# A two-layer diffusion block: layer 0's FFN in one pass over all tokens, or in two passes, context first

## The chip, the cores and the metric

The kernel runs on one core of a Trainium2 chip. The metric is the device time of one execution in microseconds (us). The core has five engines with a queue of instructions each: PE (matmuls; its weight loads are listed as PEld), DVE (vector), ACT (activations, casts, copies), POOL (a second vector engine) and SP, which here issues nearly all DMAs. An engine takes its instructions strictly in order: one that waits holds up all behind it.

## The reference

Two layers over 512 latent and 256 context tokens of width 1024. Each layer is a mixer (layer 0: windowed attention with a sink beside a dense grouped one; layer 1: differential attention) and a SwiGLU FFN with 2816 hidden columns. Before each mixer and each FFN stands an RMS norm with a shift and a scale, behind each a gate; these six vectors per layer ("modulation", parts 0 to 5) come from the conditioning vectors. Only the latents are returned, so layer 1 computes no FFN for the context.

```python
for l in range(DEPTH):
    mx = silu(c) @ mod_w[l] + mod_b[l]; mc = silu(c_ctx) @ mod_w[l] + mod_b[l]
    shx1, scx1, gx1, shx2, scx2, gx2 = split(mx, 6)    # the same for mc
    x = x + gx1 * mixer(rms(x) * (1 + scx1) + shx1, ...)
    x = x + gx2 * swiglu(rms(x) * (1 + scx2) + shx2, ffn_w_in[l], ffn_w_out[l])
    # the context likewise with mc, but in layer 0 only
def swiglu(h, w_in, w_out):
    gate, up = split(h @ w_in, 2)
    return (silu(gate) * up) @ w_out
```

## The kernel before

Tokens lie in six tiles of 128: t = 0 to 3 are latents, 4 and 5 the context. Every fp32 operand of a matmul is split into a high and a low fp32r part, and every product is three matmuls (high·high, low·high, high·low). ACT casts the high part (wbh, wdh, hdh), DVE or POOL subtracts it for the low part (wbl, wdl, hdl). Weights are loaded by SP as fp32 into raw buffers (wgr, wur, wr, wdr, modw) first.

The stages follow one another: layer 0's mixer, its FFN ("FFN 0"), layer 1's mixer ("mixer 1"), FFN 1. The normed tokens stand transposed in SBUF, latents as hT (512 columns), context as hTc (256).

**FFN 0** is the function `ffn`. It goes over the 22 slices f of 128 hidden columns in pairs p. For each f it forms gate (pg) and up (pu) products over eight K tiles, latents and context side by side (L814), then the hidden tile `silu(pg) * pu`, split. After every pair (the last two pairs together) the down products dps (L869 to L871) go over all tokens, and `residual` (L439, L440) multiplies by the gate row g and adds to the token tile x in SBUF. At the end `done0` stores the latents' tiles to `out` and norms all six for layer 1.

**Modulation.** `mod_chunk` does 256 columns on PE: two loads modw of 512 KB, eight matmuls `mod` (L184), a copy on ACT, two transposes `modcol` (L192). `mod_chunks_by_pool` (L197) does the same sum on ACT (scaling by the conditioning value, L213) and POOL (additions, L214 to L219), and leaves PE only a row product (L224) and a small transpose (L232). Layer 0's 24 chunks go on PE: most beside the start and mixer 0, the four of part 5 (FFN 0's gate) inside FFN 0's first pair. All 24 of layer 1 are done by POOL within FFN 0; `MODS1` says how many beside each pair.

**FFN 1** is `ffn_by_blocks`, latents only. For f 0 to 3 it works as above. From f = 4 on it replaces the eight half-by-half block products of a 2 x 2 split (K halves by token halves, both for gate and up together) by seven products of sums, as in Strassen's scheme: `Weights` builds sums of weight blocks (`sums1` to `sums4`, tiles ws, on POOL, ACT, DVE), `Context` (`tt.terms`, `tt.split`) the sums of token blocks (tf, tc, t3h, t3l) once, `Tile.product` issues the seven products of 12 matmuls of width 256 each, `Tile.after` combines the results (u, v, w, q) on DVE and ACT. Down products run in groups between the block products and are added up in SBUF without the gate; the tokens themselves wait in `out` in DRAM and come back at the end (`resumed`), where gate and residual are applied. Its engines are `Pinned`: these instructions keep the order of the program text.

**Order.** Elsewhere a scheduler of the framework sorts the instructions of each engine by its own estimate, within the dependencies; tile pools with few buffers set when a load may start. SP's queue is the one that the loads of weights, of modulation weights and the stores share.

## Time and profile before

| | us |
|---|---|
| median of three runs (lowest, highest) | 1775.26 (1773.18, 1776.93) |
| profiled execution | 1773.26 |
| its span | 1771.4 |
| PE busy in the span | 1696.1 |
| FFN 0, first product to the start of layer 1's first projections | 428.18 to 1008.30 |
| mixer 1 | 1008 to 1414 |
| FFN 1 | 1414 to 1771 |

PE is busy in 96% of the span, the other engines in 46 to 60%. A group row of the profile gives line, engine, operation, what is written and read, shapes and count, then busy time and the mean ns of one, then the idle time of the engine just before and what ended it. A row of a timeline gives start and length in us. Matmuls are pipelined, so their recorded lengths overlap: what one costs is the distance from start to start.

### The profile page before, as it was taken

Reading aid. Unit: us, or ns where it says so; the run is one execution under the profiler, and the core shown is the slowest. Engines: PE = TensorE matmul, PEld = TensorE weight load, DVE = VectorE, ACT = ScalarE, POOL = GpSimd, SP = SyncE. Lnnn points to the kernel's source line nnn. Section 1 sums busy time; section 2 is a strip of 40 time slices with the busy share of each in tenths; the row PEclk is TensorE's granted clock in tenths of the full one; section 3 lists DMA queues with packets and bytes.
Section 4 is the critical chain, followed back from the end, with each engine's and each line's share of the span. In section 5 each row is a group of like instructions: output and inputs, shape, how many; then the busy total and the mean of one; then the engine's idle time right before and its main releaser. Section 6 shows DMA issues by size and latency. Waiting matters only on the chain. (4 is left out here: it accounts for less than half of the span.)

```text
span 1771.4 us, 28187 instructions
## 1 busy us (share of the span) xinstructions
PE 1696.1 (96%) x10606; PEld 1471.0 (83%) x10606; DVE 1066.9 (60%) x1891; ACT 852.4 (48%) x1841; POOL 822.4 (46%) x1087
## 2 busy tenths in 40 slices
PE   6999999989999999999999999999988999999998
PEld 3887777767888888888888889999986798999997
DVE  4776555444365565554552665666664478877777
ACT  6556565443354444433332466666664345444441
POOL 2753333422054443312230657767772247777770
PEclk8999999999999999999999999999998999999999
DMA  9212233303443334433332211111122325333332
GB/s 319 55 43 73 84 96 108 107 25 119 143 144 97 105 108 155 131 110 108 105 119 62 94 37 36 37 36 51 43 84 83 96 72 161 92 95 107 107 96 95
DMA packets 176168, 169.96 MB, mean 96 GB/s; under 512 B 16608, under 2 KB 162592, under 8 KB 176032
## 3 DMA queue, kind: packets, MB, share of 16 engines
q1 hardware_dynamic: 175680, 167.96, 30.8%
q8 instruction: 83, 1.36, 0.3%
q14 instruction: 53, 0.43, 0.1%
q10 hardware_dynamic: 352, 0.21, 0.0%
HBM read 161.82 MB, written 6.32 MB: 95 GB/s over the span
## 5 line engine op out<-in xcount | busy, mean ns | idle before, releaser
L432 PE MATMUL inps<-wih,hT 128*128 128x384 f32 x384 | 132.9, 346 | 2.1 <-ACT qkv L630 2.0
L439 DVE TENSOR_TENSOR dps<-dps,g 128x512 f32<-128x512 f32 x128 | 87.8, 696 | 72.0 <-PE dps L871 57.6
L434 PE MATMUL inps<-wih,hT 128*128 128x384 f32 x384 | 130.8, 341 | 0.0
L433 PE MATMUL inps<-wil,hT 128*128 128x384 f32 x384 | 130.7, 340 | 0.0
L814 PE MATMUL pg<-hT,wgh 128*128 128x512 f32 x352 | 129.8, 392 | 0.0
L814 PE MATMUL pu<-hT,wuh 128*128 128x512 f32 x352 | 129.4, 391 | 0.4 <-DVE x L440 0.4
L213 ACT ACTIVATE modw<-modw,cols 128x256 f32<-128x256 f32 x192 | 82.0, 498 | 84.1 <-DMA modw<-in_mod_w_dram 80.4
L869 PE MATMUL dps<-wdh,hdh 128*128 128x512 f32 x264 | 106.3, 404 | 1.6 <-DVE x L440 1.6
L870 PE MATMUL dps<-wdl,hdh 128*128 128x512 f32 x264 | 104.5, 396 | 0.0
L871 PE MATMUL dps<-wdh,hdl 128*128 128x512 f32 x264 | 101.8, 396 | 0.0
L214 POOL TENSOR_TENSOR modw<-modw 128x512 f32<-128x512 f32 x48 | 62.1, 1294 | 84.5 <-ACT modw L213 84.5
L814 PE MATMUL pg<-hTc,wgh 128*128 128x256 f32 x352 | 98.1, 282 | 2.7 <-ACT hTc L308 2.4
L814 PE MATMUL pu<-hTc,wuh 128*128 128x256 f32 x352 | 97.8, 282 | 0.0
L321 POOL TENSOR_TENSOR wil<-wir,wih 128x256 fp32r<-128x256 f32 x84 | 68.2, 839 | 62.7 <-ACT wih L334 50.0
L886 PE MATMUL pg<-hT,wbh 128*128 128x256 f32 (+1 forms) x464 | 88.6, 288 | 1.6 <-DVE pg L886 1.6
L886 POOL TENSOR_TENSOR wbl<-ws,wbh 128x256 fp32r<-128x256 f32 x72 | 58.8, 847 | 64.2 <-PE pu L886 54.3
L440 DVE TENSOR_TENSOR x<-x,dps 128x512 f32<-128x512 f32 x128 | 85.2, 682 | 2.3
L552 ACT ACTIVATE Pt<-sc,nm 128x256 f32<-128x256 f32 (+3 forms) x96 | 68.0, 712 | 38.1 <-DVE nm L548 14.7
L886 POOL TENSOR_TENSOR ws<-wr 128x256 f32<-128x256 f32 x72 | 77.1, 1092 | 12.6 <-DMA wr<-in_ffn_w_in_dram 12.6
L886 PEld LDWEIGHTS pg<-hT,wbh 128*128 128x128 f32 x464 | 74.0, 188 | 6.2 <-DVE pg L886 1.8
L814 PEld LDWEIGHTS pg<-hT,wgh 128*128 128x128 f32 x352 | 66.0, 188 | 14.9 <-ACT sg L842 0.4
L814 PEld LDWEIGHTS pu<-hT,wuh 128*128 128x128 f32 x352 | 66.0, 188 | 14.9 <-issue 0.8
(332 smaller groups left out, 5507.1 us busy)
## 6 DMA issues: line engine op xcount, KB each, us to landing
modw<-in_mod_w_dram SPq DMA_DIRECT2D x96, 512.0 KB, 4.4
wdr<-in_ffn_w_out_dram SPq DMA_DIRECT2D x44, 512.0 KB, 3.7
wr<-in_ffn_w_in_dram SPq DMA_DIRECT2D x44, 512.0 KB, 5.2
wir<-in_od_w_in_dram SPq DMA_DIRECT2D x96, 128.0 KB, 2.3
wgr<-in_ffn_w_in_dram SPq DMA_DIRECT2D x22, 512.0 KB, 4.3
wur<-in_ffn_w_in_dram SPq DMA_DIRECT2D x22, 512.0 KB, 3.5
x<-in_x_dram SPq DMA_DIRECT2D x8, 512.0 KB, 6.8
wir<-in_ev_w_in_dram SPq DMA_DIRECT2D x16, 256.0 KB, 2.7
```

Of the source, the lines that this page charges most:

```text
L213: nc.scalar.activation(pr[:, k], w[:, k], AF.Copy, scale=cols[:, kk:kk + 1])
L321: nc.gpsimd.tensor_sub(lo[c], raw[c], hi[c])
L432: nc.tensor.matmul(ps, hs[0][:, k, :], a, start=k == 0, stop=False)
L433: nc.tensor.matmul(ps, hs[0][:, k, :], b, start=False, stop=False)
L434: nc.tensor.matmul(ps, hs[1][:, k, :], a, start=False, stop=k == KT - 1)
L439: nc.vector.tensor_mul(tmp, ps, g[:, n * 512:(n + 1) * 512])
L440: eng.tensor_add(xt[:, n * 512:(n + 1) * 512], xt[:, n * 512:(n + 1) * 512], tmp)
L814: nc.tensor.matmul(ps[:, s0:s1], a, cols_T(b, s0, s1)[:, k, :], start=k == 0 and q == 0, stop=k == KT - 1 and q == 2)
L869: nc.tensor.matmul(ps, hh, a, start=j == 0, stop=False)
L870: nc.tensor.matmul(ps, hh, b, start=False, stop=False)
L871: nc.tensor.matmul(ps, hl, a, start=False, stop=j == nj - 1)
L886: return tc.keep_in_program_order(op(*args, **kw))
```

## The change

FFN 0 is now `ffn_by_blocks` too, with a first pass for the context alone. **Pass 1** goes over all 22 f with the 256 context columns, plain products, down sums kept in SBUF (cacc). **Pass 2** goes over the 22 f again for the latents: f 0 and 1 plain, f 2 to 21 by seven block products. Every FFN weight of layer 0 is loaded, cast and split twice. Between the passes the context's result is gated on POOL and parked in DRAM (cx), and comes back near the end (`back`) to be normed for layer 1.

The last block of mixer 0 takes the token tiles in the order 0, 1, 2, 4, 5, 3, so that tile 3 is the last of the output projection; the norms of tiles 2 and 3 and the four chunks of part 5 of layer 0 move into pass 1, behind f = 0 in the text (`middle(0)`). The latents' tiles are stored to `out` already before pass 1's products. Modulation of layer 1: parts 0 to 2 (12 chunks) by POOL within pass 1, where for chunks with two streams the second stream's scaling moves from ACT to POOL; parts 3 to 5 (12 chunks) go on PE in mixer 1, one after each of the first three token tiles of heads 1 to 4. The output projection's weights now lie in the buffers of the FFN's blocks; `ffn` is gone; `resumed` works on POOL instead of DVE.

SP, from the end of layer 0's output projection to the FFN's first loads. x is a token tile, wor/wdr/wgr/wur/wr are weights; out_dram<-x is the store of a tile. Before:

```order
L341 DMA x_4046<-in_x_dram 128x1024
L327 DMA wgr<-in_ffn_w_in_dram 128x4x256 x2
L341 DMA x_4203<-in_x_dram 128x1024
L341 DMA x_4380<-in_x_dram 128x1024
L341 DMA x_4549<-in_x_dram 128x1024
L341 DMA x_4682<-in_ctx_dram 128x1024
L341 DMA x_4763<-in_ctx_dram 128x1024
L327 DMA wur<-in_ffn_w_in_dram 128x4x256 x2
```

With the change:

```order
L352 DMA x_4638<-in_ctx_dram 128x1024
L352 DMA x_4751<-in_x_dram 128x1024
L1593 DMA out_dram<-x_4388 128x1024
L1593 DMA out_dram<-x_4751 128x1024
L844 DMA wr<-in_ffn_w_in_dram 128x8x128 x8
L898 DMA wdr<-in_ffn_w_out_dram 128x1024
L186 DMA modw<-in_mod_w_dram 128x4x256
L844 DMA wr<-in_ffn_w_in_dram 128x8x128 x2
L898 DMA wdr<-in_ffn_w_out_dram 128x1024
L186 DMA modw<-in_mod_w_dram 128x4x256
```

The first FFN weights (then wgr, now wr) stood ahead of the last token loads; now they stand behind the four stores of latent tiles, of which the last (x_4751) is tile 3.

SP a little later, in pass 1 (L186 is a load for PE's chunks, L214 for POOL's):

```order
L186 DMA modw<-in_mod_w_dram 128x4x256 x6
L214 DMA modw<-in_mod_w_dram 128x4x256 x2
L844 DMA wr<-in_ffn_w_in_dram 128x8x128 x2
L898 DMA wdr<-in_ffn_w_out_dram 128x1024
L214 DMA modw<-in_mod_w_dram 128x4x256 x4
L844 DMA wr<-in_ffn_w_in_dram 128x8x128 x2
L898 DMA wdr<-in_ffn_w_out_dram 128x1024
L214 DMA modw<-in_mod_w_dram 128x4x256
L844 DMA wr<-in_ffn_w_in_dram 128x8x128 x2
```

Between the weights wr of one f and those of the next now stand two, then four, then single loads modw.

PE, the chunks of part 5 of layer 0. Before, one of the four places:

```order
L814 MATMUL pu<-hTc_4656,wul 128x256
L192 MATMUL modcol<-cst,modr 128x128 x2
L184 MATMUL mod<-modw,s_pad 32x256 x8
L869 MATMUL dps<-wdh,hdh 128x512
L870 MATMUL dps<-wdl,hdh 128x512
L871 MATMUL dps<-wdh,hdl 128x512
```

With the change (pu is f = 2 of pass 1, npt the transposes of tile 3's norm):

```order
L824 MATMUL pu<-hTc_4495,wbl 128x256
L310 MATMUL npt<-cst,nh 128x128 x4
L192 MATMUL mod<-modw,s_pad 32x256 x8
L200 MATMUL modcol<-cst,modr 128x128 x2
L192 MATMUL mod<-modw,s_pad 32x256 x8
L200 MATMUL modcol<-cst,modr 128x128 x2
L192 MATMUL mod<-modw,s_pad 32x256 x8
L200 MATMUL modcol<-cst,modr 128x128 x2
L824 MATMUL dps<-wdh,hdh 128x512
L824 MATMUL dps<-wdl,hdh 128x512
L824 MATMUL dps<-wdh,hdl 128x512
L824 MATMUL dps<-wdh,hdh 128x512
L824 MATMUL dps<-wdl,hdh 128x512
```

Before, one chunk stood between products; now three chunks follow one another, and the fourth comes 22 products later.

PE in mixer 1, one of the twelve new places (sc are attention scores, ppt transposes of probabilities, av the sums of values):

```order
L662 MATMUL qpt<-identr,qd 128x128 x4
L668 MATMUL kpt<-identr,kd 128x128 x2
L192 MATMUL mod<-modw,s_pad 32x256 x8
L704 MATMUL ppt<-cst,e 128x128 x6
L685 MATMUL sc<-kT,qt 128x512
L686 MATMUL sc<-kT,qt 128x512
L685 MATMUL sc<-kT,qt 128x512
L686 MATMUL sc<-kT,qt 128x512
L200 MATMUL modcol<-cst,modr 128x128 x2
L712 MATMUL av<-vv,PT 128x128 x4
```

The chunk's eight matmuls stand between two steps of the attention, its transposes some matmuls later.

```diff
--- before.py
+++ after.py
 PBUF = 4
 MODS0 = (0, 2, 2, 0)
-MODS1 = (2, 2, 2, 2, 2, 3, 3, 4, 4, 0)
+MODS1 = (0, 1, 1, 1, 1, 1, 1, 1, 2, 3, 0)
+LAST_ORDER = (0, 1, 2, 4, 5, 3)
...
                     pr = pool.tile([P, 4, width], F32, name="modp", tag="mp", bufs=1) if i else w
                     for k in range(4):
                         kk = 8 * i + 4 * pc + k
-                        nc.scalar.activation(pr[:, k], w[:, k], AF.Copy, scale=cols[:, kk:kk + 1])
+                        if i:
+                            nc.gpsimd.tensor_scalar(pr[:, k], w[:, k], cols[:, kk:kk + 1], 1.0, ALU.mult, ALU.mult)
+                        else:
+                            nc.scalar.activation(pr[:, k], w[:, k], AF.Copy, scale=cols[:, kk:kk + 1])
...
-    def ffn(l, xs, ntok, wp, fp, done, mods=()):
...
-    def ffn_by_blocks(l, xs, p_fb, new_blocks, new_down, fp, rooms, done):
+    def ffn_by_blocks(l, xs, p_fb, new_blocks, new_down, fp, wr, rooms, done, ctx_part=None):
...
-                raw = fp.tile([P, KT, P], F32, name="wr", tag="wr", bufs=4)
+                raw = wr.tile([P, KT, P], F32, name="wr", tag="wr", bufs=4)
...
+                if n == 8 and ctx_part:
+                    ctx_part.back()
...
+        class Plain:
+            def __init__(self, f):
+                gate, up = load(f)
+                self.raws = [*up, *gate]
+                self.w = []
+            def hi(self, a=nc.scalar):
+                self.w.append(block())
+                a.copy(self.w[-1][0], self.raws[len(self.w) - 1])
+            def lo(self):
+                hi, lo = self.w[-1]
+                dve.tensor_sub(lo, self.raws[len(self.w) - 1], f32(hi))
+        def ctx_group(t, n, keep):
+            turn["sum"] = (turn["sum"] + 1) % 4
+            ps = p_1.tile([P, 512], F32, name="dps", tag=("acc0", "tr0", "acc1", "tr1")[turn["sum"]])
+            for j in range(2):
+                down_part(ps, chid[j], cwd[j], t, n, j == 0, j == 1)
+            acc = cacc[t][:, n * 512:(n + 1) * 512]
+            if keep:
+                nc.scalar.copy(acc, ps)
+            yield
+            if not keep:
+                dve.tensor_add(acc, acc, ps)
+        if ctx_part:
+            width = TOK - SEQ
+            cacc = [fp.tile([P, D], F32, name="cacc", tag="cacc", bufs=2) for _ in range(2)]
+            ct = [[hT[z][1][:, k * half:(k + 1) * half, :] for z in range(2)] for k in range(2)]
+            chid, cwd = [], []
+            cur = Plain(0)
+            for _ in range(4):
+                cur.hi()
+                cur.lo()
+            last = None
+            four = [(t, n) for t in range(2) for n in range(2)]
+            for f in range(NF):
+                nxt = Plain((f + 1) % NF)
+                d = down(f, cwd)
+                next(d)
+                two = [ctx_group(*tn, f < 4) for tn in four[f % 2 * 2:f % 2 * 2 + 2]] if f > 1 else []
+                ps = [p[:, :width] for p in places()]
+                for i in range(2):
+                    product(ps[0], cur.w[i], ct[i], i == 0, i == 1)
+                nxt.hi()
+                if last:
+                    next(last)
+                nxt.lo()
+                if last:
+                    end(last)
+                for g in two[:1]:
+                    next(g)
+                nxt.hi()
+                nxt.lo()
+                for i in range(2):
+                    product(ps[1], cur.w[2 + i], ct[i], i == 0, i == 1)
+                for g in two[:1]:
+                    end(g)
+                next(d)
+                nxt.hi()
+                nxt.lo()
+                for g in two[1:]:
+                    next(g)
+                last = hidden(ps, nc.scalar, dve, None, chid)
+                next(last)
+                next(d)
+                nxt.hi()
+                nxt.lo()
+                end(d)
+                for g in two[1:]:
+                    end(g)
+                if f % 2 and f > 1:
+                    del chid[:2], cwd[:2]
+                if f % 2 == 0:
+                    ctx_part.middle(f // 2, fp)
+                cur = nxt
+            g1 = gate_row(l, 5, 1, fp)
+            nxt = Plain(1)
+            downs = [down(0), down(1)]
+            for d in downs:
+                next(d)
+            ps = places()
+            for i in range(2):
+                product(ps[0], cur.w[i], rows[i], i == 0, i == 1)
+            nxt.hi(act)
+            next(last)
+            nxt.lo()
+            end(last)
+            nxt.hi(act)
+            nxt.lo()
+            two = [ctx_group(*tn, False) for tn in four]
+            for g in two[:2]:
+                next(g)
+            for d in downs:
+                end(d)
+            tt.terms()
+            for i in range(2):
+                product(ps[1], cur.w[2 + i], rows[i], i == 0, i == 1)
+            for _ in range(2):
+                nxt.hi(act)
+                nxt.lo()
+            for g in two[2:]:
+                next(g)
+            for g in two:
+                end(g)
+            for t in range(2):
+                pool.tensor_mul(cacc[t], cacc[t], g1)
+                pool.tensor_add(cacc[t], cacc[t], xs[NTX + t])
+            fp = ctx_part.end(cacc)
+            rest = hidden(ps, act, dve)
+            next(rest)
+            next(rest)
+            end(rest)
+            xs = [keep.tile([P, D], F32, name=f"acc{t}", tag="xo", bufs=6) for t in range(NTX)]
+            w = Weights(2)
+            todo.extend((w, i) for i in range(7))
+            cur = nxt
+            ps = places()
+            for i in range(2):
+                product(ps[0], cur.w[i], rows[i], i == 0, i == 1)
+            w.sums1()
+            w.sums2()
+            w.sums3()
+            tt.split()
+            for _ in range(4):
+                hi()
+                lo()
+            for i in range(2):
+                product(ps[1], cur.w[2 + i], rows[i], i == 0, i == 1)
+            w.sums4()
+            for _ in range(3):
+                hi()
+                lo()
+            last = Rest(hidden(ps, act, dve))
+            next(last.rest)
+            tt.split_last()
+            nxt = Weights(3)
+            nxt.sums1()
+            nxt.sums2()
+            first = 2
...
-                dve.tensor_mul(xs[t], xs[t], g)
-                dve.tensor_add(xs[t], xs[t], xr)
+                pool.tensor_mul(xs[t], xs[t], g)
+                pool.tensor_add(xs[t], xs[t], xr)
...
-        order = CTX_FIRST if b < 3 else tuple(range(NT))
+        order = CTX_FIRST if b < 3 else LAST_ORDER
...
-            ws = [Pool("w0u", "right"), Pool("w0d", "right")]
+            blocks = Pool("w0b", "right")
+            downs = Pool("w0d", "right")
+            new_block, new_down = block_rooms(blocks.pool, 8), down_rooms(downs.pool)
...
+    sc_pool.__exit__(None, None, None)
+    fb_pool = block_banks()
+    wr = Pool("wr0")
+    parts = [(1, part, n, 2 if part < 2 else 1) for part in range(3) for n in range(4)]
+    class CtxPart:
+        def middle(self, p, pool):
+            if p == 0:
+                with tc.issue_after(chain[nc.tensor]):
+                    for t in LAST_ORDER[2:]:
+                        if t < NTX:
+                            norm_hT(t, xs[t], 0, 1, pool, (("mw", 2), ("mp", 1)))
+                for n in range(4):
+                    mod_chunk(0, 5, n, lambda shape, name: pool.tile(shape, F32, name=name, tag="mw", bufs=2), pool,
+                              f"tr{n % 2}", room=("ma", 4))
+                return
+            if p == 2:
+                for t in range(NTX):
+                    nc.sync.dma_start(out[0, t * P:(t + 1) * P, :], xs[t])
+            n = MODS1[p]
+            if n:
+                mod_chunks_by_pool(parts[:n], pool)
+                del parts[:n]
+        def end(self, acc):
+            nonlocal fp
+            self.cx = [dram.tile([P, D], F32, name=f"cx{j}", tag=f"cx{j}") for j in range(2)]
+            for m, t in zip(self.cx, acc):
+                nc.sync.dma_start(m, t)
+            fp.close()
+            fp = Pool("ffn0")
+            for z in "hl":
+                fp.pool.tile([P, SEQ], F32R, name=f"hd{z}", tag=f"hd{z}", bufs=4)
+            return fp.pool
+        def back(self):
+            open_ctx()
+            for j, m in enumerate(self.cx):
+                xt = wr.pool.tile([P, D], F32, name="cxb", tag="wr", bufs=4)
+                nc.sync.dma_start(xt, m)
+                norm_hT(NTX + j, xt, 1, 0, wr.pool, (("wr", 4), ("wr", 4)))
...
+    ffn_by_blocks(0, xs, fb_pool.__enter__(), new_block, new_down, fp.pool, wr.pool,
+                  [lambda j=j: new_room0(j) for j in range(3)], done0, CtxPart())
...
+            if 1 <= h <= 4 and t < 3:
+                mod_chunk(1, 3 + (3 * h + t - 3) // 4, (3 * h + t - 3) % 4, raw_tile, at.pool, "acc0")
```

More of the change, by code (lines that the diff above doesn't have):

```diff
@@ L877, in backbone @@
+    chain = {}
     class Pinned:
@@ L1203, in ffn_by_blocks @@
         hid, wd = [], []
-        first = first_pair()
-        w2 = [[halves(r, act, dve) for r in raw] for raw in load(2)]
-        end(hidden(first[0], act, dve, first_hid))
-        for t in range(NTX):
-            nc.sync.dma_start(out[0, t * P:(t + 1) * P, :], xs[t])
-        downs = [down(0), down(1)]
-        for d in downs:
-            next(d)
-        w3 = [[halves(r, act, dve) for r in raw] for raw in load(3)]
-        end(hidden(first[1], act, dve))
+        pending = [(t, n) for t in range(NTX) for n in range(2)]
         def plain(ws):
@@ L1293, in ffn_by_blocks @@
         last_two(w, nxt, dns, last)
-        for half_ in range(2):
-            four = pending[half_ * 4:half_ * 4 + 4]
-            open_ = [p_1.tile([P, 512], F32, name="dps", tag=("acc0", "tr0", "acc1", "tr1")[i]) for i in range(4)]
-            if half_ == 0:
+        for part in range(2):
+            four = pending[part * 4:part * 4 + 4]
+            open_ = [p_1.tile([P, 512], F32, name="dps", tag=f"acc{i}") for i in range(2)]
+            open_.extend(places())
+            if part == 0:
                 for ps, (t, n) in zip(open_, four):
@@ L1455, in backbone @@
                     next(proj)
-            for _ in range(MODS0[b] if t % 2 or not proj else 0):
+            for _ in range(MODS0[b] if i % 2 or not proj else 0):
                 if mods:
```

310 lines of the change are left out of this document (135 added, 175 removed).

## The prediction

> **What bounds the kernel now.** I read the page's shares first, then a table by stage, then single stretches. The page says which engine is full:
>
> ```profile
> PE 1696.1 (96%) x10606; PEld 1471.0 (83%) x10606; DVE 1066.9 (60%) x1891; ACT 852.4 (48%) x1841; POOL 822.4 (46%) x1087
> ```
>
> By stage, from the windows view (length, then busy time of PE, PEld, DVE, ACT, POOL, clock, DMA share, GB/s): FFN 0, mixer 1, FFN 1.
>
> ```profile
> 428.18:1008.30 580.12, 575.53 (x3136) 486.45 (x3135) 304.90 (x425) 233.00 (x423) 190.32 (x196) 1.00 0.37 117
> 1008.00:1400.00 392.00, 369.12 (x2402) 341.63 (x2401) 235.52 (x467) 230.86 (x588) 240.45 (x411) 0.98 0.17 50
> 1414.00:1771.00 357.00, 348.81 (x2337) 319.26 (x2337) 280.74 (x433) 145.92 (x252) 221.10 (x222) 1.00 0.36 105
> ```
>
> FFN 0 idles 580.12 − 575.53 = 4.6 us: it is bound by its matmul count alone, so any work taken from PE there is worth its time, and any new wait costs its time. Mixer 1 idles 22.9 us. FFN 1, which already uses block products, idles 8.2.
>
> A matmul's price is the distance between starts, not its recorded duration. Timeline of PE, 20 down products of width 512 (first and last), and of SP, four loads wdr, one per block round of FFN 1 (first and last):
>
> ```profile
> 849.63 0.39 PE L870 MATMUL dps<-wdl,hdh 128*128 128x512 f32 x1
> 854.08 0.39 PE L871 MATMUL dps<-wdh,hdl 128*128 128x512 f32 x1
> 1546.60 0.34 SPq L957 DMA_DIRECT2D wdr<-in_ffn_w_out_dram  x1
> 1592.85 0.34 SPq L957 DMA_DIRECT2D wdr<-in_ffn_w_out_dram  x1
> ```
>
> Width 512: 4.45/19 = 0.234 us. A block round: 46.25/3 = 15.4 us for 24 products of width 512 and 84 of 256, hence width 256: (15.4 − 5.6)/84 = 0.117. FFN 1 therefore keeps PE full at these prices, and the DVE and ACT work of a block round fits under it.
>
> **What it removes.** The latents' up products are 44 × 24 = 1056 of width 512 (247.1 us). After: f 0 and 1 plain, 96 × 0.234 = 22.5; f 2 to 21 by blocks, 20 × 84 × 0.117 = 196.6. Saved: 28.0. Context products (1056 × 0.117) and down products (792 × 0.234) keep count and width: the second pass costs PE nothing, only a second read of the weights. The old stage's 4.6 us of idle time goes too; what takes its place is counted below. Twelve of POOL's 24 modulation chunks lose their row products (32 to 20 matmuls): 12 × 0.117 = 1.4. Together −34.0.
>
> **A. Start of the context pass.** Before, the first FFN weights were loaded ahead of the last sums. Now SP's order is: store of x tile 3, then the first wr. That store waits for tile 3's residual on DVE, the last act of the output projection; all eight wr loads wait behind it, and behind them ACT's casts, DVE's wbl, and PE. The start of FFN 1 has the same steps:
>
> ```profile
> 1406.28 4.53 SPq L904 DMA_DIRECT2D wr<-in_ffn_w_in_dram  x4
> 1412.45 0.70 DVE L439 TENSOR_TENSOR ops<-ops,g 128x512 f32<-128x512 f32 x1 [0.49 <-PE ops L755]
> 1413.06 0.40 DVE L306 TENSOR_SCALAR nhc<-npt,aff,modc 128x128 f32<-128x128 f32 x1
> 1413.38 0.68 DVE L440 TENSOR_TENSOR x<-x,ops 128x512 f32<-128x512 f32 x1
> 1413.86 1.12 ACT L913 CAST wbh<-wr 128x512 fp32r<-128x512 f32 x2
> 1414.51 0.50 PE L920 MATMUL pg<-hT,wbh 128*128 128x256 f32 x2 [1.23 <-ACT wbh L913]
> 1415.95 0.58 PE L920 MATMUL pg<-hT,wbl 128*128 128x256 f32 x1 [0.94 <-DVE wbl L914]
> ```
>
> Issue to first product is 8.2 us. There it lies under 6 us of output products; here nothing lies over it. The residual before it is 2 × (0.70 + 0.68) = 2.8 and three small norm steps among it 3 × 0.4. PE has only 8 transposes for this time, some 0.6. So 4.0 + 0.4 (store) + 8.2 − 0.6 = 12. Bounds: 8 (the first cast needs half the queue) to 15 (eight loads share the DMA).
>
> **B. Half clock.** In the same place the granted clock fell:
>
> ```profile
> 1416.00:1418.00 2.00, 2.00 (x9) 2.00 (x10) 1.90 (x4) 2.00 (x6) 1.70 (x3) 0.50 0.52 199
> 1418.00:1420.00 2.00, 2.00 (x14) 2.00 (x13) 1.91 (x3) 2.00 (x5) 1.12 (x1) 0.67 0.90 263
> ```
>
> About 3 us at half clock: 1.5 us lost per long wait where PE then has work. I take 2 in all, 0 to 5. The Trainium skill (TensorE: Matmul & The Clock Gate, Part 1) says that an idle window of about 3.4 us halves the clock and about 3.4 us of busy time restores it. The row agrees, though here waits of 1.23 and 0.94 sufficed; by the rule A and each wait of C would lose up to 1.7 more, 5 to 7 in all instead of 2.
>
> **C. The four chunks of layer 0's modulation (part 5).** Before, each stood between products. Now three stand in a row on PE: 8 mod matmuls, 2 transposes, three times, and a fourth 22 products later. Their weights have two buffers; the loads of the next chunk wait until PE has read the last one, and SP's next FFN loads stand behind them.
>
> ```profile
> modw<-in_mod_w_dram SPq DMA_DIRECT2D x96, 512.0 KB, 4.4
> 468.38 0.38 PE L192 MATMUL modcol<-cst,modr 128*128 128x128 f32 x2
> 468.69 1.07 PE L184 MATMUL mod<-modw,s_pad 128*32 128x256 f32 x16
> 207.87 1.07 PE L184 MATMUL mod<-modw,s_pad 128*32 128x256 f32 x16 [1.08 <-DMA modw<-in_mod_w_dram]
> ```
>
> A chunk is 1.45 us of PE (its last transposes cost that before too); a load takes 4.4. The first chunk's second half is requested only after tile 3's transposes just ahead of it: 4 us bare. Each later chunk: 4.4 less the 1 us in which the previous one ends, 3.4, for two chunks; the fourth has 3.3 us of products over it and waits about 0.5. Sum 11; 7 to 15.
>
> **D. The context pass itself.** Per f: 48 × 0.117 + 12 × 0.234 = 8.4 us of PE. The other engines' rows (FFN 1, then POOL in FFN 0):
>
> ```profile
> L886 DVE TENSOR_TENSOR wbl<-wr,wbh 128x512 fp32r<-128x512 f32 x54 | 45.2, 842 | 6.4 <-ACT wbh L886 6.4
> L886 DVE TENSOR_TENSOR wdl<-wdr,wdh 128x512 fp32r<-128x512 f32 x37 | 32.6, 894 | 0.3 <-ACT wdh L886 0.3
> L886 ACT CAST wbh<-wr 128x512 fp32r<-128x512 f32 x56 | 34.3, 619 | 28.6 <-PE pg L886 11.7 <-PE pu L886 10.7 <-PE pg L920 5.4
> L214 POOL TENSOR_TENSOR modw<-modw 128x512 f32<-128x512 f32 x48 | 62.1, 1294 | 84.5 <-ACT modw L213 84.5
> L219 POOL TENSOR_TENSOR ma<-ma,modw 128x256 f32<-128x256 f32 x24 | 22.1, 920 | 1.3
> L293 POOL TENSOR_SCALAR nh<-x,rs_n 128x1024 f32<-128x1024 f32 x5 | 6.7, 1334 | 0.4
> ```
>
> DVE: 4 × 0.84 + 2 × 0.89 + three operations of half that width, 1.3, = 6.4, under 8.4; ACT less. POOL, per two-stream chunk: 4 × 1.29 + 6 × 0.9 + eight new scalings of width 256, by the last row about 0.33 each = 13.2, under the 16.8 of its two f. One place is tight: after C, SP's order has two modw, the wr of f 6, then four modw, and only then the wr of f 7. The last of the four waits until POOL has done nearly two chunks, about 33 us after C by 13.2 each; f 7 is due on PE at about 38, less 6 for load and cast. I take 3; 0 (scalings cheaper) to 14 (priced like an addition, 0.9, a chunk is 18).
>
> **E. The turn to the latents.** DVE must form the seven block operands before the products of f 2:
>
> ```profile
> L886 DVE TENSOR_TENSOR tf<-tf,hT 128x1024 f32<-128x1024 f32 x4 | 6.6, 1645 | 0.1
> ```
>
> Seven such sums are 11.5 us, with splits and weight sums between, against 22.5 us of plain products, where DVE also prepares weights. 4.5; 0 to 11.5.
>
> **F. Block rounds** as in FFN 1, but with 8 block buffers for 9 and no long run-in: 1; 0 to 5. **G. End of FFN 0**: layer 1's first weights queue behind the acc stores on SP, PE has the last groups: 3; 0 to 6.
>
> **H. Twelve chunks in mixer 1**, three in each of heads 1 to 4: 12 × 1.45 = 17.4 us of PE. They stand among attention steps whose waits total 22.9 us in the stage; a part falls into these. 14; 6 to 17.
>
> Sum: −34.0 + 12 + 2 + 11 + 3 + 4.5 + 1 + 3 + 14 = **+16.5**. The profiled execution took 1773.26 (span 1771.4 and 1.9 around it), the median is 1775.26: 1789.8 against the one, **1791.8** against the other. I forecast 1791, slower.
>
> **Rivals.**
> *Mixer 1's idle time takes H whole.* The 22.9 us exceed 17.4, and mixer 0's chunks waited little (the 1.08 above). Then the sum is +2.5, and it decides once the start (A, B, C, 25 together) costs under 22: at their low ends, 15, the result is −7.5, 1768, **faster**. Against it: the waits of mixer 1 are many and short, and a chunk delays what stands behind it. 0.25.
> *POOL and SP bind the context pass* (D at 14, A and C high): a two-stream chunk of 18 us against 16.8 holds up every wr behind its modw. +16.5 + 11 + 4 = 1807. For it: POOL's additions are its dearest rows; against it: the last row above. 0.15.
> *The gains just pay for the waits*: H whole in idle time and the rest as summed: within 0.2% (3.5 us, about what a measurement can tell from no change), 1778. 0.07.
> That the block products don't save PE time is excluded by the 15.4 us round of FFN 1.
>
> **How the numbers follow.** The forecast's own range, 1780 to 1803, gets 0.53. With the faster case at 1768 and the POOL case at 1807 the range is 1763 to 1811. Faster 0.25, same 0.07, slower 0.68.
>
> **What would show it.** A: PE idle some 12 us after the last ops, ended by wbh. C: waits of about 3.4 before mod, ended by modw. D: ACT or DVE idle on wr in mid pass, POOL full. H: mixer 1 longer by 12 to 17 us at equal idle time; if its idle time falls by as much, the first rival is right. FFN 0's products must total about 528 us against 555. I am wrong if PE's idle time in FFN 0 stays under 20.

## The result and the profile after

The changed kernel takes 1904.56 us (median of 4 runs, 1902.31 to 1907.06) against 1774.22 in the same runs before: a ratio of 1.074 (95% interval 1.071 to 1.076), 130 us slower. The forecast was 1791, slower: the sign was right, the size was not, and 1904.56 lies far outside the range. The profiled span is 1901.6 us.

The page's busy times by engine:

```profile
PE 1732.4 (91%) x11518; PEld 1522.8 (80%) x11518; DVE 1211.9 (64%) x2188; ACT 924.9 (49%) x1991; POOL 1091.3 (57%) x1358
```

The windows view of the three stages FFN 0, mixer 1 and FFN 1 (length, then busy time of PE, PEld, DVE, ACT, POOL, clock, DMA share, GB/s):

```profile
429.00:1081.50 652.50, 575.79 (x3822) 515.94 (x3821) 455.12 (x709) 297.70 (x556) 435.50 (x448) 0.93 0.48 146
1081.50:1542.00 460.50, 416.43 (x2702) 374.59 (x2700) 246.80 (x514) 250.23 (x626) 248.95 (x424) 0.94 0.25 77
1542.00:1901.60 359.60, 349.57 (x2337) 320.21 (x2337) 279.24 (x423) 145.45 (x251) 241.84 (x230) 0.99 0.35 104
```

The same three stages of the kernel before, cut at the same events:

```profile
428.18:1008.30 580.12, 575.53 (x3136) 486.45 (x3135) 304.90 (x425) 233.00 (x423) 190.32 (x196) 1.00 0.37 117
1008.30:1414.50 406.20, 382.11 (x2467) 352.13 (x2466) 243.64 (x483) 237.26 (x601) 243.61 (x415) 0.98 0.18 54
1414.50:1771.40 356.90, 348.81 (x2337) 319.26 (x2337) 280.24 (x431) 145.42 (x251) 221.10 (x222) 0.99 0.36 105
```

FFN 0 is 72.4 us longer, mixer 1 54.3, FFN 1 2.7. PE's idle time in FFN 0 went from 4.6 to 76.7 us, and in mixer 1 from 24.1 to 44.1. FFN 0 has the same busy time as before although it has 28 us less work at full clock: its clock fell from 1.00 to 0.93, that of mixer 1 from 0.98 to 0.94. What PE computes at half clock behind a long wait is a second price of that wait.

**The start of FFN 0.** Timeline of PE (start, length, what, and the idle time before it with its releaser), the five long waits before the context pass runs steadily:

```profile
441.18 0.80 PE L824 MATMUL pu<-hTc,wbh 128*128 128x256 f32 x2 [11.13 <-ACT wbh L1171]
467.11 1.93 PE L192 MATMUL mod<-modw,s_pad 128*32 128x256 f32 x16 [6.84 <-ACT nhc L315]
473.76 1.94 PE L192 MATMUL mod<-modw,s_pad 128*32 128x256 f32 x16 [3.54 <-DMA modw<-in_mod_w_dram]
480.87 1.94 PE L192 MATMUL mod<-modw,s_pad 128*32 128x256 f32 x16 [4.00 <-DMA modw<-in_mod_w_dram]
509.33 1.06 PE L235 MATMUL modrow<-ma,cst 128*32 128x256 f32 x4 [13.26 <-POOL ma L230]
```

Timeline of SP, two of the issues behind which the first and the third of them stand:

```profile
433.77 14.41 SPq L844 DMA_DIRECT2D wr<-in_ffn_w_in_dram  x8
468.25 14.98 SPq L186 DMA_DIRECT2D modw<-in_mod_w_dram  x6
```

The first four stand where terms A and C put them. The second ends otherwise than predicted: not by a load, but by the norm of tile 3 on ACT (nhc), which stands on ACT behind a cast that itself waits 3.1 us for its weights wr. The chunks ran at half clock: 1.93 us for the 16 records of eight matmuls that took 1.07 before. The fifth was not predicted: the row product of POOL's first chunk stands in PE's order, and all slices behind it wait until POOL is done.

**The context pass.** The gate's activation `sg` on ACT comes once per slice f; its starts give the pace. Timeline of ACT, f = 2, f = 3 and f = 21:

```profile
492.08 0.38 ACT L873 ACTIVATE sg<-pg 128x256 f32<-128x256 f32 x1
518.41 0.38 ACT L873 ACTIVATE sg<-pg 128x256 f32<-128x256 f32 x1
...
701.04 0.39 ACT L873 ACTIVATE sg<-pg 128x256 f32<-128x256 f32 x1 [3.29 <-PE pg L824]
```

One step of 26.3 us, then 18 of 10.1 in the mean, where 8.4 were priced. POOL's groups in 441 to 702 (busy time, mean ns, idle time before):

```profile
L222 POOL TENSOR_SCALAR modp<-modw,cols 128x256 f32<-128x256 f32 x64 | 42.4, 681 | 56.2 <-DMA modw<-in_mod_w_dram 56.1
L225 POOL TENSOR_TENSOR modw<-modw 128x512 f32<-128x512 f32 x24 | 34.0, 1418 | 18.0 <-ACT modw L224 18.0
L225 POOL TENSOR_TENSOR modp<-modp 128x512 f32<-128x512 f32 x16 | 21.3, 1333 | 1.1
L227 POOL TENSOR_TENSOR ma<-modw 128x256 f32<-128x256 f32 x12 | 11.6, 964 | 0.3
```

PE's two largest waits in 515 to 702 (total, times, longest), of 14.8 us in all:

```profile
PE dps L824 <- ACT hdh L878: 10.3, 6, 2.5
PE modcol L243 <- ACT ma L240: 3.9, 2, 2.6
```

Both end at ACT. ACT's own largest wait in the same stretch:

```profile
ACT modw L224 <- POOL modp L222: 33.9, 15, 4.7
```

And ACT's timeline in one of these:

```profile
541.63 1.41 ACT L224 ACTIVATE modw<-modw,cols 128x256 f32<-128x256 f32 x3 [3.57 <-POOL modp L222]
542.95 0.35 ACT L878 CAST hdh<-pu 128x256 fp32r<-128x256 f32 x1
```

A two-stream chunk is 8 × 0.68 + 4 × 1.38 + 6 × 0.98 (the mean of its additions of width 256, one group of which is shown) = 16.8 us of POOL: exactly its two slices (2 × 8.4), with nothing left for any wait. ACT scales the first stream in place (L224), so it has to wait until POOL's new scaling has read the same buffer (L222), and the hidden tile's cast hdh, for which PE's down products wait, stands behind it on ACT.

**The turn to the latents**, 702.2 to 754.3: its work is 128 products of width 512 and some 37 of 256, 34.3 us at the prices used, so 18 are lost, 13 of them in three waits and the rest at half clock:

```profile
734.68 0.80 PE L824 MATMUL pg<-hT,wbh 128*128 128x256 f32 x2 [4.26 <-ACT wbh L824]
738.33 0.58 PE L824 MATMUL pg<-hT,wbl 128*128 128x256 f32 x1 [2.85 <-DVE wbl L824]
750.34 0.80 PE L824 MATMUL dps<-wdh,hdh 128*128 128x512 f32 x1 [5.87 <-ACT hdh L824]
```

**The block rounds** behind it run as priced: loads wdr at 759.28 and 1021.21, 17 rounds apart, 15.4 us each.

**Mixer 1.** PE's longest wait in 1082 to 1480 (total, times, longest):

```profile
PE inps L444 <- POOL wil L332: 18.6, 13, 1.9
```

The turn of one head on PE's timeline:

```profile
1205.36 0.39 PE L444 MATMUL inps<-wil,hTc 128*128 128x256 f32 x1 [1.61 <-POOL wil L332]
1208.26 0.58 PE L444 MATMUL inps<-wil,hTc 128*128 128x256 f32 x1 [1.78 <-POOL wil L332]
1211.70 0.58 PE L444 MATMUL inps<-wil,hTc 128*128 128x256 f32 x1 [1.59 <-POOL wil L332]
```

And the windows of these 12 us:

```profile
1202.00:1206.00 4.00, 2.04 (x16) 1.70 (x15) 1.76 (x4) 2.34 (x5) 3.84 (x8) 1.00 0.35 98
1206.00:1210.00 4.00, 2.22 (x9) 1.62 (x8) 0.54 (x2) 0.87 (x2) 2.78 (x6) 0.77 0.47 130
1210.00:1214.00 4.00, 1.95 (x8) 1.55 (x8) 0.41 (x2) 0.83 (x4) 3.62 (x6) 0.50 0.56 179
```

The first context projections of a head wait three times for the head's own weights (wil) that POOL is just making. The clock falls after the first two of these waits: by windows of one microsecond it is 1.00 up to 1208, 0.59 in the next and 0.50 from 1209 on, so that the third wait and the products behind it fall into half clock. None of this stood in the prediction: it priced the chunks, not what they do to the order around them.

### The profile page after: what moved, and what is told of

It reads as the page before. It is cut to its first block, busy times and chain, and to the rows that moved or that the text cites. A ratio compares the mean times of both kernels' runs of the same rounds, so it can differ in the third digit from the quotient of the medians.

```text
span 1901.6 us, 31186 instructions
## 1 busy us (share of the span) xinstructions
PE 1732.4 (91%) x11518; PEld 1522.8 (80%) x11518; DVE 1211.9 (64%) x2188; ACT 924.9 (49%) x1991; POOL 1091.3 (57%) x1358
## 5 line engine op out<-in xcount | busy, mean ns | idle before, releaser
L824 PE MATMUL pg<-hT,wbh 128*128 128x256 f32 (+1 forms) x976 | 189.0, 291 | 11.6 <-DVE pg L824 4.8
L824 DVE TENSOR_TENSOR wbl<-wr,wbh 128x512 fp32r<-128x512 f32 x218 | 186.0, 858 | 14.5 <-ACT wbh L824 8.5
L824 PEld LDWEIGHTS pg<-hT,wbh 128*128 128x128 f32 x976 | 158.1, 191 | 21.8 <-DVE pg L824 5.0
L824 POOL TENSOR_TENSOR ws<-wr 128x256 f32<-128x256 f32 x152 | 156.1, 1048 | 15.2 <-DMA wr<-in_ffn_w_in_dram 15.2
L824 ACT CAST wbh<-ws 128x512 fp32r<-128x512 f32 x152 | 91.5, 626 | 129.8 <-PE pg L824 67.7
L824 PE MATMUL pg<-hT,wbl 128*128 128x256 f32 (+1 forms) x488 | 141.6, 290 | 2.8 <-DVE wbl L824 2.8
L824 DVE TENSOR_TENSOR wdl<-wdr,wdh 128x512 fp32r<-128x512 f32 x132 | 126.0, 961 | 1.2 <-ACT wdh L824 1.2
L824 PEld LDWEIGHTS pg<-hT,wbl 128*128 128x128 f32 x488 | 93.3, 191 | 4.6 <-DVE wbl L824 3.1
L824 POOL TENSOR_TENSOR ws<-ws,wr 128x256 f32<-128x256 f32 x76 | 87.8, 1174 | 0.0
L824 DVE TENSOR_TENSOR wbl<-ws,wbh 128x512 fp32r<-128x512 f32 x76 | 80.1, 1054 | 11.8 <-ACT wbh L824 11.8
L444 PE MATMUL inps<-wil,hTc 128*128 128x256 f32 (+1 forms) x192 | 68.3, 356 | 21.1 <-POOL wil L332 18.6
```

Of the source, the lines that this page charges most:

```text
L444: nc.tensor.matmul(ps, hs[0][:, k, :], b, start=False, stop=False)
L824: ins = op(*args, **kw)
```

## The experiments

All times are medians of four runs, with the ratio to the kernel before, measured beside them on the same chip, and its 95% interval. Theories are lettered anew in each expectation; "term A" and so on are the prediction's.

### Mixer 1 without its chunks

```diff
-            if 1 <= h <= 4 and t < 3:
-                mod_chunk(1, 3 + (3 * h + t - 3) // 4, ..., "acc0")
```

> Leaves out the twelve chunks of layer 1's modulation in mixer 1 (parts 3 to 5 are filled with a constant); all else as changed (1904.6 us). Theory A (the six loads modw of a head stand before the next head's twelve loads wir in SP's queue and in the two raw buffers; PE then waits for the weights and falls to half clock): the whole difference of mixer 1 goes, 45 to 55 us, so 1850 to 1860, and the waits of inps for POOL's wil fall from 18.6 us to below 3. Rival B (the chunks cost their PE time only, 12 x 1.45 = 17; mixer 1 is longer for another reason): 1887, and the waits for wil stay.

1846.36 us, 1.040 (1.038 to 1.043): 58 us gone for 17.4 us of PE work. PE's waits for wil, 18.6 us with the chunks, are down to 0.4, and mixer 1 is back at its old length:

```profile
1079.40:1487.40 408.00, 383.87 (x2487) 354.02 (x2484) 245.50 (x486) 243.66 (x614) 248.47 (x424) 0.98 0.19 57
```

### The context pass without POOL's chunks, and with their loads alone

```diff
-MODS1 = (0, 1, 1, 1, 1, 1, 1, 1, 2, 3, 0)
+MODS1 = (0,) * 11
```

> Leaves out the twelve chunks that POOL does in the context pass (parts 0 to 2 of layer 1 are filled with a constant); all else as changed. Theory A (POOL's chunks hold back SP's queue, ACT, and PE at the row product): the context pass from its fourth slice on comes down from 189 to about 165 us and the 13.3 us wait goes: 35 to 45 us off, 1860 to 1870. Rival B (loading, casting and splitting every weight twice binds the pass by itself, DVE or DMA): only the 13 us wait and the row products go, 1888, and the pass keeps a pace of about 10 us per slice.

1855.53 us, 1.046 (1.044 to 1.048): 49 us gone. For the second kernel the call of `mod_chunks_by_pool` is replaced by its two loads a chunk into the same buffers:

> Pass 1 with the 24 loads modw of POOL's chunks, but without their scalings, additions and row products (parts 0 to 2 filled with a constant). Theory A (computing binds, not the loads): as without the chunks, 1855 to 1860. Rival B (DMA traffic and SP's order bind): at least 20 of the 49 us stay, 1875 or more.

1856.18 us, 1.047 (1.045 to 1.049): the loads, their traffic and their places in SP's queue cost nothing, as long as nothing holds the buffers that they fill. It is the computing. Window of 135 us of the context pass with the chunks, and DVE's first group in it:

```profile
515.00:650.00 135.00, 122.20 (x831) 107.60 (x830) 93.21 (x131) 79.71 (x166) 123.03 (x129) 0.97 0.68 206
```

```profile
L824 DVE TENSOR_TENSOR wbl<-wr,wbh 128x512 fp32r<-128x512 f32 x49 | 49.0, 1001 | 0.0
```

The same without the chunks (the first of the two kernels), and the timeline of ACT at f = 2, f = 3 and f = 20:

```profile
515.00:650.00 135.00, 135.00 (x965) 126.36 (x964) 90.42 (x161) 64.77 (x112) 1.56 (x1) 1.00 0.60 188
```

```profile
L824 DVE TENSOR_TENSOR wbl<-wr,wbh 128x512 fp32r<-128x512 f32 x64 | 43.7, 683 | 0.0
```

```profile
492.03 0.38 ACT L873 ACTIVATE sg<-pg 128x256 f32<-128x256 f32 x1
501.81 0.38 ACT L873 ACTIVATE sg<-pg 128x256 f32<-128x256 f32 x1
644.76 0.38 ACT L873 ACTIVATE sg<-pg 128x256 f32<-128x256 f32 x1
```

Without the chunks PE has no idle time at all and the pace is 8.41 us (142.95 over 17 slices), the price of term D. With them POOL is 91% busy, and DVE's subtraction takes 1.00 us instead of 0.68: POOL slows DVE too. PE's waits that end at DVE itself are only 0.6 us in 515 to 702; what the slower DVE costs by itself was not tested.

### Two cures for the context pass

The second stream's scaling goes back from POOL to ACT (`nc.scalar.activation` for both streams):

> Undoes one line of the change: the second stream's scaling of POOL's chunks goes back from POOL to ACT. As changed, a two-stream chunk measures 16.9 us on POOL (eight scalings of 0.68 among them), as long as the two slices it stands beside, and ACT waits 45 us in all for POOL before it may scale the first stream in place. Theory A (this chain of POOL and ACT binds pass 1): a chunk falls to about 11.5 us on POOL, ACT's wait goes, 30 to 40 us off, 1865 to 1875. Rival B (the loads modw in SP's queue, or DVE slowed while POOL works, bind it): 10 us off at most, 1894 or more. Rival C (ACT then is late with the casts): no gain or slower.

1907.18 us, 1.076 (1.074 to 1.079): no gain. POOL's busy time falls, ACT's rises, and PE is where it was:

```profile
515.00:650.00 135.00, 123.95 (x816) 110.32 (x817) 86.04 (x126) 97.31 (x215) 87.34 (x79) 0.94 0.64 195
```

The wait only changed its end: POOL now waits for ACT's scalings (21.9 us in this stretch). Next POOL issues its own loads, so that SP does not stand behind POOL's buffers:

```diff
-                nc.sync.dma_start(w, mod_w[l, ...])     # in mod_chunks_by_pool
+                nc.gpsimd.dma_start(w, mod_w[l, ...])
```

> The loads modw of POOL's chunks in pass 1 are issued from POOL's own queue instead of SP's; the computing is unchanged. SP waited 61 us in pass 1 for POOL to free one of two buffers modw, with the next FFN weights wr behind that. Theory A (this wait at the head of SP's queue is what passes POOL's time on to PE): 25 to 45 us off, 1860 to 1880. Rival B (ACT's scaling in place behind POOL, and DVE's splits at 0.93 us instead of 0.68 while POOL works): within 10 us of 1904.6.

1915.76 us, 1.081 (1.078 to 1.084): 11 us slower. An issue takes POOL 0.79 us, 19 us for the 24 loads, which it does not have, and DVE's subtraction now takes 1.19 us. What SP's waiting behind POOL's buffers costs is therefore not seen by itself: a gain of some us could be hidden under this. Groups in 515 to 690:

```profile
L214 POOL DMA_DIRECT2D modw<-in_mod_w_dram x21 | 16.5, 787 | 1.8 <-POOL ma L227 0.9 <-POOL ma L230 0.9
L824 DVE TENSOR_TENSOR wbl<-wr,wbh 128x512 fp32r<-128x512 f32 x62 | 74.1, 1194 | 0.0
```

### Half of POOL's chunks

Six chunks, the four with two streams in every second pair of slices: `MODS1 = (0, 1, 0, 1, 0, 1, 0, 1, 1, 1, 0)`.

> Six of the twelve chunks that POOL computes in the context pass are left out (four of the eight with two streams, two of the four with one; the rest of layer 1's modulation is filled with constants), and the six come in pairs of slices with no chunk between them. All twelve cost 49 us (1904.6 against 1855.5 without them). Theory S (saturation): a two-stream chunk takes POOL 16.9 us where its two slices take PE 16.84, so with a free pair behind each chunk the delay is caught up: 1856 to 1870, at least 35 of the 49 us gone. Rival L (each chunk costs its share, whatever its neighbours): half of the 49 us, 1877 to 1883.

1888.69 us, 1.063 (1.061 to 1.066): 16 of the 49 us gone, less than either theory. Timeline of ACT, f = 2, 3, 5, 6 and 21:

```profile
494.77 0.38 ACT L873 ACTIVATE sg<-pg 128x256 f32<-128x256 f32 x1
521.14 0.38 ACT L873 ACTIVATE sg<-pg 128x256 f32<-128x256 f32 x1
538.57 0.38 ACT L873 ACTIVATE sg<-pg 128x256 f32<-128x256 f32 x1
553.34 0.38 ACT L873 ACTIVATE sg<-pg 128x256 f32<-128x256 f32 x1
686.27 0.38 ACT L873 ACTIVATE sg<-pg 128x256 f32<-128x256 f32 x1 [3.23 <-PE pg L824]
```

The 49 us have two parts. One comes once: 26.4 instead of 9.8 us before f = 3 (the row product that waits for POOL's first chunk) and 14.8 instead of 8.4 before f = 6 stand here as in the full kernel (26.3 and 15.7). That is 24 us in the full kernel. The other is the pace behind it: 132.9 us for the last 15 slices, against 148.6 with all chunks and 125.8 without any. So of this part, 23 us, two thirds went with half the chunks: there saturation comes nearer than a price per chunk, for the first part it fell.

### Layer 0's part 5 in mixer 0 again

`MODS0 = (1, 2, 2, 1)`: the four chunks go beside mixer 0 instead of between f = 0 and f = 2.

> The four chunks of part 5 of layer 0 go into mixer 0 (15 chunks in its head groups and one in the last block) instead of the context pass. Theory A (their serial loads stop PE: 16 us of waits from 460 to 484 us and half clock behind them, and they delay POOL's first chunk): 20 to 30 us off, 1875 to 1885. Rival B (the same wait comes back one step later, at POOL's first row product): at most 6 us off, 1898 or more.

1886.33 us, 1.063 (1.061 to 1.066): 18 us gone. The first product of FFN 0 comes 9.0 us later (450.20 instead of 441.18: the chunks' price in mixer 0), but f = 1 to f = 2 takes 14.6 instead of 33.7, and the row product of POOL's first chunk waits less:

```profile
493.77 1.07 PE L235 MATMUL modrow<-ma,cst 128*32 128x256 f32 x4 [7.07 <-POOL ma L230]
```

It was 13.26, so the four chunks had also held up POOL's first chunk. At their place in the change they cost 19 us, and some 6 more by this wait. PE's wait for tile 3's norm (nhc) is still 5.6 us here, where no chunk stands behind it: most of the 6.84 above belongs to the norm and not to the chunks.

### Mixer 1: neither place, loads nor bank

The twelve chunks spread over seven heads, at a head's end and the next one's beginning (two a head, one in the first and the last):

> Same twelve chunks in mixer 1, but two per head instead of three, placed right behind the next head's loads (fourth token tile of one head, first of the next), so that SP reaches the next loads wir half a head earlier. Theory A (queue order): the waits for wil nearly go, mixer 1 loses 25 to 30 us, 1875 to 1880. Rival B (PE time and the clock, whatever the place): within 4 us of 1904.6.

1894.05 us, 1.066 (1.063 to 1.070): 10 us gone, less than theory A and more than its rival. The twelve chunks without their loads (a constant tile as operand):

> The twelve chunks in mixer 1 keep their matmuls, copies and transposes but read a constant tile instead of loading 1 MB each (parts 3 to 5 are wrong values then). Theory A (the loads in SP's queue and in the two raw buffers hold up the weights wir): only PE's 17 us and little more stay of the 58, 1863 to 1872. Rival B (the chunks' places among the attention steps, PE waits and half clock): most of the 58 stays, 1890 or more.

1897.77 us, 1.070 (1.068 to 1.072): 7 us. The chunk in the other accumulator bank, where the projections do not stand:

> In mixer 1 the twelve chunks put their sums (mod, modcol) into PSUM bank acc1 instead of acc0. acc0 is the only bank of layer 1's projections (inps): in PE's order no inps stands between a chunk's mod and its modcol, and the projections come in bunches behind the attention instead of between its steps. Theory A (the chunk blocks the projections' bank, PE then waits on the attention's latencies and falls to half clock): 15 to 35 us off, 1870 to 1890. Rival B (twelve extra dependent steps cost this much in any bank; acc1 is shared with av): within 8 us of 1904.6.

1905.38 us, 1.075 (1.073 to 1.077): nothing. PE's order is another here, with attention steps between the groups of context products, and its waits for wil fall from 18.6 to 5.7 us (those for wih rise from 1.5 to 5.8); the price stays all the same. The chunk's products alone, without the copy, the transposes and what follows:

> Mixer 1's twelve chunks keep their loads and their eight products each, but not the copy on ACT, the two transposes, the sum and the addition behind them (the values are constants). Theory K (the chain product, copy, transposes holds PE's accumulator bank and PE's order until ACT comes): at least 35 of the 58 us go, 1870 or less. Rival M (the products in the order are enough): only the transposes' own 4.6 us and little else go, 1890 to 1901.

1900.14 us, 1.070 (1.067 to 1.072): the transposes' own 4.6 us and no more. And the twelve chunks in the kernel before, with the other twelve left to POOL in its one-pass FFN (`MODS1 = (1, 1, 1, 1, 1, 2, 2, 3, 0, 0)`):

> The kernel before, with only one part of the change: parts 3 to 5 of layer 1's modulation on PE in mixer 1 at the same twelve places, POOL keeps parts 0 to 2. Theory A (queue and raw buffers in mixer 1, whatever FFN 0 does): plus 50 to 58 us, 1823 to 1831. Rival B (it costs so much only behind the two passes): plus 17 at most, 1790.

1822.33 us, 1.028 (1.026 to 1.030): 50 us slower than before, with 19.3 us of waits for wil. The price has nothing to do with the two passes.

### Mixer 1: one chunk per head

> Four of mixer 1's twelve chunks, one in each of heads 1 to 4, the other eight left out and filled with constants. Twelve cost 58 us (1904.6 against 1846.4). Rival L (a price per chunk, 4.8 us each): 1846.4 + 19 = 1866, 1861 to 1870. Theory O (one chunk in a head already breaks up the order by which the next head's context projections come behind their weights; the price is per head): at least two thirds of the 58 stays, 1885 or more. Theory T (a threshold: one chunk, 1.45 us of PE work, fits into the idle time of a head): under 1856.

1880.34 us, 1.059 (1.057 to 1.061): four chunks cost 34 us, 8.5 each, where twelve cost 58: between theories L and O, and T fell. The distance from one head to the next, read on ACT's timeline at the first projection copy of a head, after and without chunks:

```profile
1213.17 0.37 ACT L641 COPY qkv<-inps 128x256 f32<-128x256 f32 x1 [3.69 <-PE inps L445]
1267.34 0.37 ACT L641 COPY qkv<-inps 128x256 f32<-128x256 f32 x1 [3.70 <-PE inps L445]
```

```profile
1238.50 0.38 ACT L641 COPY qkv<-inps 128x256 f32<-128x256 f32 x1
1278.94 0.38 ACT L641 COPY qkv<-inps 128x256 f32<-128x256 f32 x1
```

Taken for four heads of each kernel (mean distance, us):

| chunks in a head | distance of heads |
|---|---|
| none | 40.5 |
| one | 46.9 |
| two (at end and beginning) | 47.4 |
| three | 53.1 |
| three, without loads | 50.8 |
| three, products alone | 51.2 |

The first chunk of a head costs 6.4 us with 1.45 us of PE work in it. Four such turns are 26 of the 34 us, and 50 of the 58; the rest lies outside them. What a chunk changes can be read in the order of PE's instructions around one turn of a head (C and L: products of context and latent projections, with their number; sc, ppt, av, qpt, kpt: attention; the bars only part the groups):

```
no chunks:     ... qpt4 kpt2 C19 | sc2 ppt6 | C5 | sc2 kpt2 av6 qpt4 | C24 qpt4 ...
one chunk:     ... sc4 av6 C13 qpt4 C6 kpt2 | C29 qpt4 ...
three chunks:  ... mod8 ppt6 modcol2 av6 L24 qpt4 kpt2 | C43 qpt4 kpt2 C5 ...
```

Without chunks the scheduler has attention work left to put between the 48 context products; with them this work has gone in ahead of, or beside, the chunk, and the 48 come as one bunch, at the moment at which their weights are cast (the timeline above). That this bunch is what costs is a reading of the order, and the other bank, where the largest groups read were 29 and 35 products with attention steps between the rest, speaks against it as the only cause.

### Mixer 1 with weights that are never late

From head 2 on, head 1's weights are used again; once without chunks, once with all twelve:

```diff
+    kept = []
...
-        ws = []
-        for u in range(4):
+        ws = [] if h < 2 else kept[0]
+        kept[:] = [ws]
+        for u in range(4 if h < 2 else 0):
```

> Mixer 1 without its twelve chunks (as in the run without them, 1846.4 us), and from head 2 on every head projects with head 1's weights: 24 loads, casts and subtractions of wi units are left out, so no projection can wait for weights. Nearly nothing waited for them there (0.4 and 0.2 us), and PE was 98% busy in mixer 1: both theories, 1836 to 1848.

> The changed kernel with all its chunks in mixer 1, and from head 2 on head 1's weights (24 loads, casts and subtractions of wi units left out); its PE order still puts a head's 48 context products in one bunch behind the chunks, as the changed kernel does. Against the run of this call without chunks: Theory W (the 58 us are the chunks' own 17.4 us of PE work and, for the rest, weights that come late to the bunch, with the half clock behind each wait): 17 to 28 us more, some 1855 to 1875. Rival P (attention's own chain of scores, exponentials and sums gets worse by the other order, whatever the weights do): 45 us more or above, 1885 to 1905.

1831.47 us (1.032, 1.030 to 1.035) and 1858.21 us (1.048, 1.046 to 1.051). The first is 15 us below the run without chunks and 5 below what was expected, although PE had waited there only 0.6 us for these weights: leaving out the loads, casts and subtractions does more than was meant. The chunks now cost 26.7 us instead of 58, although the bunch is still in PE's order. Mixer 1 without and with chunks:

```profile
1084.00:1474.20 390.20, 375.51 (x2487) 350.80 (x2485) 236.25 (x486) 229.25 (x590) 194.09 (x352) 0.98 0.12 35
```

```profile
1084.20:1500.30 416.10, 395.42 (x2701) 359.57 (x2699) 241.95 (x513) 231.80 (x601) 195.43 (x352) 0.98 0.20 63
```

The clock is 0.98 in both, idle time 14.7 and 20.7. Heads stand 39.8 and 44.8 us apart: three chunks cost 5 us, little over their 4.35 us of PE work. So of the 58 us some 27 are the chunks and their disturbance of attention, and 31 need each head's own weights to be loaded, cast and split. By the waits above these 31 are weights that come late, with the half clock behind the waits; but the two kernels also have less work on ACT, POOL and the queue, and this part was not separated from it.

### What the two passes are worth by themselves, and a combination

> All 24 chunks of layer 1's modulation are left out, in the context pass and in mixer 1 (constants in their place): the two-pass FFN with nothing moved into or beside it, except that part 5 of layer 0 still stands at its start. If the two prices add up: 1904.6 - 49 - 58 = 1797, 1792 to 1802, so still some 24 us above the kernel before, which computes all of the modulation. If the two-pass FFN by itself were a gain: under 1773.

1800.87 us, 1.014 (1.013 to 1.016). The two prices add to within 4 us (1904.6 − 49 − 58 = 1797), and with layer 1's modulation for nothing the two-pass FFN is still 26 us slower than the kernel before, which computes all of it. Last, three of the moves together (part 5 in mixer 0, the other bank, POOL's own loads):

> Part 5 in mixer 0 (e4, 18 us off) together with the two edits of e9 and e10. If the three places are independent the gains add up: 1904.6 - 18 - 25 - 35 = about 1827 by theory A of both; 1886 by the rivals of both.

1906.10 us, 1.075 (1.073 to 1.078): the 18 us that the first gains alone do not survive beside the third, which alone loses 11. No combination here comes near the old time. The run without layer 1's modulation says why: even if the 18 us of part 5 came off it too, an estimate from two runs, it would stand at 1783, still 8 above the kernel before.

## Why the prediction was wrong in size

It priced nearly every term on PE and found the other engines covered. By its own terms:

| term | predicted | measured |
|---|---|---|
| removed work | −34.0 | −34: block rounds 15.4 us as priced |
| A. start of the pass | 12 (8 to 15) | 12.2 (429.0 to 441.2, 11.1 of it one wait ended by wbh) |
| B. half clock | 2 (0 to 5) | 8: behind A 2.9 (f = 0's products took 8.5 us for 5.6), behind C's waits some 5 |
| C. part 5's chunks | 11 (7 to 15) | 16 in waits, 6.8 of them ended by tile 3's norm; 19 by the run, with their own PE time and half clock |
| D. the context pass | 3 (0 to 14) | 49 (209.0 us for 19 slices priced at 160) |
| E. turn to the latents | 4.5 (0 to 11.5) | 18 |
| F. block rounds | 1 (0 to 5) | 3 (two waits in the last rounds, 1.9 and 0.8, ended by DVE) |
| G. end of FFN 0 | 3 (0 to 6) | 5 |
| H. chunks in mixer 1 | 14 (6 to 17) | 54 in the stage, 58 by the run |

The measured column, with C as 16 and H as 54, sums to 131; with 2.7 in FFN 1 that is 3 more than the 130. D's 49 holds the PE time of POOL's row products, part of which the stage had before too.

**Right**: the removed work, A with its length and its releaser (wbh), the two waits before mod ended by modw (3.5 and 4.0), and the sign. What it named as the sign of being wrong, PE idle under 20 us in FFN 0, did not come: it was 76.7. C's first wait is where it was put, but its reason was another, the norm on ACT.

**D failed** at two steps. The chunk was priced at 13.2 us of POOL with a scaling at 0.33, a quarter of a row four times as wide; it took 0.68, and a chunk 16.8. The upper bound, 18 a chunk, did contain that, but then only SP's queue was followed (late weights, +11): ACT waited 9.1 us for wr in 515 to 702, and 33.9 for POOL. What ended PE's waits were PE's own row product in PE's order (13.3 us once) and then ACT, whose in-place scaling stands behind POOL's read with the hidden tile's cast behind it. DVE's sum was too small as well: it left out the two additions of the down sums (2 × 0.68), and the subtractions went from 0.68 to 1.00 us, so that DVE had some 8 us of work in a slice of 8.4. The rival "POOL and SP bind the context pass" had the right engine, and a price of 11 + 4 on top of the sum where 46 was due; SP's part of it no run decides: loads alone lose nothing, and POOL's own loads are 11 us slower, though that run also adds POOL's time for the issues.

**H failed** because it counted a chunk's PE time against the stage's idle time. The idle time was not free to be filled: it rose by 20 us instead, to 44, and what PE computed was stretched by the clock. By the runs some 27 of the 58 us are the chunks and their disturbance of attention, and 31 come only where every head has its own weights; how much of this is the order that no longer covers the turn of heads stays open, since in the other bank the order was better and the price the same. The faster rival (idle time takes H whole) fell by the same fact.

**E failed** on what is late. The prediction looked at DVE's seven sums (11.5 us); PE waited for casts of weights on ACT (4.3), their subtraction on DVE (2.9) and the first latent hidden tile (5.9), and then ran at 0.6 of the clock. The same waits stand in the run without any modulation of layer 1 (4.3, 2.9 and 6.0), so they belong to the two passes.

**B and the clock**: the row in the prediction gave 1.5 us per long wait, 2 in all. Behind A the clock stood at 0.50 until 447.0, for 5.8 us of work; behind C's waits each chunk took 2.6 us instead of 1.45, and PE came back to full clock only at 488. The prediction's second estimate, 5 to 7 by the rule of the Trainium skill (TensorE: Matmul & The Clock Gate, Part 1), was nearer to the 8 measured. That the clock falls only after an idle window of about 3.4 us does not hold here as a rule for single waits: in mixer 1 two waits of 1.61 and 1.78 us, with 1.1 us of work between them, brought it from 1.00 to 0.50.

What stays open: why the slice before f = 6 costs the same with half the chunks was not tested (for the first row product the run with part 5 in mixer 0 shows that it waits less when POOL's loads come earlier); what makes the other bank as dear as the first; and the 9 us that the chunks cost beyond their PE time where weights are never late were not taken apart.

## What to carry to other kernels

Where work goes to an engine "with room", price a whole unit of it against the whole period in which it must be done, waits included, and look for the places at which another engine's in-order queue meets it: at 16.8 of 16.8 us each small fix only handed the wait to the next engine. Idle time on the bound engine in a stage of many short waits is not a store to fill: one chunk of 1.45 us cost 6.4, with an order on PE in which less attention work covered the turn of the weights. And price a wait twice on PE: once as idle time, once as the half clock behind it.

## What was not expected of the hardware

- A scaling of 256 columns on POOL takes 0.68 us where one of 1024 takes 1.33: by these two rows a fixed part of 0.46 us and 0.85 ns per column.
- POOL's work (its scalings and additions) slows DVE's subtractions of two SBUF tiles from 0.68 to 1.00 us, while DVE's additions that read PSUM keep 0.68 (the `cacc` groups: 678 and 687 ns with and without chunks). The Trainium skill (SBUF — State Buffer, Who interferes with whom) has this rule: a DVE instruction with two SBUF inputs contends with a POOL instruction that reads SBUF, one with at most one such input, outside DVE's two-port modes, does not. The trace agrees.
- A load issued by POOL costs it 0.79 us of its own time; the same load issued by SP costs POOL nothing.
